# A row softmax over 32,768 columns: half rows moved in one 64 KB transfer per partition instead of two of 32 KB

## The chip, the core and the metric

The kernel runs on one core of one Trainium2 chip. The core has a vector engine (DVE), a scalar engine (ACT) and a sync engine (SP) that are used here, and 16 DMA engines that move data between HBM, where input and output lie, and the core's on-chip memory, which has 128 partitions. TensorE does nothing in this kernel, and GpSimd writes four constants at the start. The metric is device time in microseconds (us) of one execution.

## The reference

```python
def setup_inputs():
    batch, seq, vocab = 16, 256, 32768
    return {"logits": np.random.randn(batch, seq, vocab).astype(np.float32), "temperature": 1.0}

def reference(logits, temperature):
    scaled = logits / temperature
    scaled = scaled - scaled.max(axis=-1, keepdims=True)
    exp_scaled = np.exp(scaled)
    return (exp_scaled / exp_scaled.sum(axis=-1, keepdims=True)).astype(np.float32)
```

There are 16 x 256 = 4,096 rows of 32,768 float32. The input is 536.87 MB and so is the output, and each has to cross between HBM and the core once.

## The kernel before

A row is cut into two halves of 16,384 elements (`_SPLIT = 2`), and each half takes one partition. So 128 partitions hold 64 rows; such a group of 64 rows is called a *tile* below, and there are 64 of them (g = 0 to 63). A half row is 64 KB.

A tile is moved in two *chunks* (`_CW = 8192`, so C = 2): each chunk is 128 partitions x 8,192 elements, 32 KB per partition, 4,096 KB (4 MiB) in all. Each chunk has a buffer of its own, and there are six (`_BUFS = 6`), 6 x 32 = 192 KB of each partition.

For each tile the kernel does three things.

- `exps`: for each *piece* of a chunk (`_PIECE = 8192`, so a piece is a whole chunk), DVE takes the negated maximum of the piece in each partition (L107), then ACT replaces the piece by exp(x - that maximum) in place and adds up the sum in the same pass (L114). Each piece is scaled by its own maximum, so ACT can begin on a piece before the rest of the row is there.
- `factors`: ten or so tiny instructions turn the maxima and sums of the pieces into one factor per piece. The two halves of a row lie in neighbouring partitions, so the partial results are exchanged between partitions (L84, L87). ACT does one tiny exp (L131), and DVE does the rest (L129 to L150).
- `scales`: each piece is multiplied by its factor in place, the first `_DVE_SHARE = 0.5` of it on DVE (L160) and the rest on ACT (L163).

In the last tile the pieces are 4,096 elements in any case. In the first and the last tile the loads go in parts of 16 KB per partition (`_LAST_DMA = 4096`), and in the last tile the stores too.

All transfers are issued by SP, on one queue, in the order that the list `order` at the end of the kernel gives: first as many loads as there are buffers, then a store of chunk 0, and from there store of chunk i, load of chunk i + 5, store of chunk i + 1, and so on (with `_BUFS = n`, load i + n - 1 follows store i). SP works through this list strictly in order. A store (L75) waits until DVE and ACT have scaled the chunk, and a load (L64) waits until the store that last read its buffer has landed. A transfer that waits holds everything behind it on SP. DVE and ACT work through their own lists, tile after tile, in the same manner.

Of the kernel before, what the change touches and what calls it, by code (L numbers as in the profile page):

```python
# [6 lines left out]


_SPLIT = 2
_CW = 8192  # L10
_BUFS = 6
_PIECE = 8192
_LAST_DMA = 4096
_DVE_SHARE = 0.5


@with_exitstack
# [211 lines left out]
```

## Time and profile before

| | |
|---|---|
| time, median of 3 runs | 2494.52 us (2493.96 to 2495.61) |
| the profiled execution's own time | 2495.61 us |
| its span, first to last instruction | 2493.8 us |
| DVE busy | 1487.4 us (60%) |
| ACT busy | 1405.0 us (56%) |
| read from and written to HBM | 536.87 MB each |
| mean rate of the DMA engines | 431 GB/s |
| a 4,096 KB store, issue to landing, median | 38.2 us |
| a 4,096 KB load, issue to landing, median | 29.0 us |

The span is 1.8 us shorter than the time of the same execution; the rest lies before its first and after its last instruction. The profile's page gives each engine's busy time, the busy share of the DMA engines in 40 slices of the span, the chain of work that ended last, followed back from the end, and groups of instructions by line of the kernel with the number of them, the busy time, the mean duration of one, and the idle time before them. The trace behind it also has a record for every packet of the DMA engines (its size, start and duration) and for each of the 16 landings of a transfer, one from each DMA engine.

### The profile page before, as it was taken

The numbers are of one execution on the slowest core, as the hardware profiler recorded it, in microseconds if no ns is written. First come the engines' busy times: TensorE is split into PE (matmuls) and PEld (weight loads), VectorE is DVE, ScalarE is ACT, GpSimd is POOL, SyncE is SP. The second block draws the span as 40 slices with busy tenths as digits, with TensorE's granted clock in tenths as the row PEclk, the third lists the DMA queues.
The fourth block names the chain that finished last, engine by engine and source line by source line (L and its number), as shares of the span: only waits on it lengthen the run. The fifth ranks groups of instructions, "written<-read, shape, count | busy, mean of one in ns | idle before, by whom it ended". The sixth has DMA issues, their size and how long they took to land.

```text
span 2493.8 us, 2234 instructions
## 1 busy us (share of the span) xinstructions
DVE 1487.4 (60%) x964; ACT 1405.0 (56%) x455; POOL 0.2 (0%) x4
## 2 busy tenths in 40 slices
DVE  7655565556655566555665566655666566655663
ACT  5665554655556555565555655555546555465553
POOL 0000000000000000000000000000000000000000
DMA  9999999999999999999999999999999999999998
GB/s 412 433 430 432 429 431 432 433 433 434 433 434 432 435 432 435 432 435 431 436 431 435 432 434 433 434 433 433 433 433 433 433 433 434 434 433 434 432 431 368
DMA packets 37745, 1073.90 MB, mean 431 GB/s; under 512 B 4192, under 2 KB 4192, under 8 KB 4192
## 3 DMA queue, kind: packets, MB, share of 16 engines
q1 hardware_dynamic: 37728, 1073.76, 99.9%
q14 instruction: 17, 0.14, 0.0%
HBM read 536.87 MB, written 536.87 MB: 431 GB/s over the span
## 4 chain that ended last, share of the span: by engine, by line
DMA 96%; SPq 1%; ACT 1%; DVE 1%; issue 1%; ACTq 0%
DMA out_dram<-xs 93%; DMA xs<-in_logits_dram 2%; SPq L64 1%; DVE nm L107 1%; ACT xs L163 1%; ACT xs L114 0%; ACTq L224 0%; SPq L75 0%; DVE f L150 0%; ACT ee L131 0%; DVE rS L149 0%; DVE Sh L87 0%; DVE ttj L138 0%; DVE Sh L84 0%; DVE Sh L138 0%
## 5 line engine op out<-in xcount | busy, mean ns | idle before, releaser
L114 ACT ACTIVATE xs<-xs,nm 128x8192 f32<-128x8192 f32 (+1 forms) x130 | 912.1, 7016 | 972.4 <-DVE nm L107 972.4
L107 DVE TENSOR_REDUCE nm<-xs 128x1 f32<-128x8192 f32 (+1 forms) x130 | 1111.6, 8551 | 527.3 <-DMA xs<-in_logits_dram 527.3
L163 ACT ACTIVATE xs<-xs,f 128x4096 f32<-128x4096 f32 (+1 forms) x130 | 468.1, 3648 | 71.4 <-DVE f L150 71.4
L160 DVE TENSOR_SCALAR xs<-xs,f 128x4096 f32<-128x4096 f32 (+1 forms) x130 | 295.7, 2318 | 3.7 <-DVE f L150 1.8
L138 DVE CUSTOM_DVE_ANT_0 ttj<-ee,ssum 128x2 f32<-128x2 f32 x64 | 10.3, 161 | 423.8 <-ACT ee L131 423.8
L114 ACT ACTIVATION_READ_ACCUMULATOR xs<-xs,nm 128x1 f32 x130 | 24.2, 186 | 0.0
L131 ACT ACTIVATE ee<-nm,nMh 128x2 f32<-128x2 f32 x64 | 17.9, 280 | 0.0
L150 DVE TENSOR_SCALAR f<-ee,rS 128x2 f32<-128x2 f32 x64 | 14.6, 229 | 2.2
L149 DVE RECIPROCAL rS<-Sh 128x1 f32<-128x1 f32 x64 | 10.5, 164 | 2.2
L87 DVE TENSOR_TENSOR nMh<-nMh 128x1 f32<-128x1 f32 x64 | 10.2, 160 | 2.2
L87 DVE TENSOR_TENSOR Sh<-Sh 128x1 f32<-128x1 f32 x64 | 10.2, 160 | 2.2
L129 DVE TENSOR_REDUCE nMh<-nm 128x1 f32<-128x2 f32 x64 | 9.9, 155 | 2.2
L84 DVE STREAM_SHUFFLE nMh<-nMh 128x1 f32<-128x1 f32 x64 | 9.7, 151 | 0.0
L84 DVE STREAM_SHUFFLE Sh<-Sh 128x1 f32<-128x1 f32 x64 | 9.7, 151 | 0.0
L114 ACT ACT_TABLE_LOAD x1 | 1.3, 1283 | 12.9 <-DMA xs<-in_logits_dram 12.9
L138 DVE DVE_READ_ACCUMULATOR2_ANT Sh<- 128x1 f32 x64 | 5.3, 84 | 0.0
L84 DVE LOAD_MASK_SELECT Sh<-Sh x64 | 0.9, 14 | 2.8
L84 DVE LOAD_MASK_SELECT nMh<-nMh x64 | 0.9, 14 | 2.7
L210 POOL MEMSET const-bfloat16-1.0<- 128x1 bf16 x1 | 0.1, 102 | 0.0
L210 POOL MEMSET const-uint8-127<- 128x1 uint8 x1 | 0.1, 102 | 0.0
L210 POOL MEMSET const-float32-0.0<- 128x1 f32 x1 | 0.1, 99 | 0.2 <-issue 0.2
L210 POOL MEMSET const-float32-1.0<- 128x1 f32 x1 | 0.1, 99 | 0.0
## 6 DMA issues: line engine op xcount, KB each, us to landing
out_dram<-xs SPq DMA_DIRECT2D x126, 4096.0 KB, 38.2
xs<-in_logits_dram SPq DMA_DIRECT2D x124, 4096.0 KB, 29.0
xs<-in_logits_dram SPq DMA_DIRECT2D x8, 2048.0 KB, 22.3
out_dram<-xs SPq DMA_DIRECT2D x4, 2048.0 KB, 26.7
```

The costliest lines, as they stand in the source:

```text
L64: nc.sync.dma_start(out=xs[:, s : s + n], in_=x[g * P : (g + 1) * P, c * CW + s : c * CW + s + n],)
L84: nc.vector.stream_shuffle(out=v[:, j + 1 : j + 2], in_=v[:, j : j + 1], mask=mask)
L87: nc.vector.tensor_tensor(out=v[:, j + 1 : j + 2], in0=v[:, j : j + 1], in1=v[:, j + 1 : j + 2], op=op,)
L107: nc.vector.tensor_reduce(out=nm[:, k : k + 1], in_=xs[:, s : s + n], axis=X, op=A.max, negate=True)
L114: nc.scalar.activation(out=xs[:, s : s + n], in_=xs[:, s : s + n], func=Exp, bias=nm[:, k : k + 1], scale=inv_t, accum_out=ssum[:, k : k + 1],
L129: nc.vector.tensor_reduce(out=nMh[:, 0:1], in_=nm, axis=X, op=A.min)
L131: nc.scalar.activation(out=ee, in_=nm, func=Exp, bias=nMh[:, n_rounds : n_rounds + 1], scale=-1.0,)
L138: nc.vector.tensor_tensor_reduce(out=ttj, in0=ee, in1=ssum, scale=1.0, scalar=0.0, op0=A.mult, op1=A.add, accum_out=Sh[:, 0:1],)
L149: nc.vector.reciprocal(out=rS, in_=Sh[:, n_rounds : n_rounds + 1])
L150: nc.vector.tensor_scalar_mul(out=f, in0=ee, scalar1=rS)
L160: nc.vector.tensor_scalar_mul(out=xs[:, s : s + cut], in0=xs[:, s : s + cut], scalar1=f[:, k : k + 1])
L163: nc.scalar.activation(out=xs[:, s + cut : s + n], in_=xs[:, s + cut : s + n], func=Copy, scale=f[:, k : k + 1],)
```

## The change

Four constants change. A chunk becomes a whole half row: 16,384 elements, 64 KB per partition, 8,192 KB per transfer, so a tile is one chunk (C = 1). There are three buffers of 64 KB in place of six of 32 KB, the same 192 KB. A piece becomes 4,096 elements, so a chunk has four pieces, each with its own maximum, sum and factor. DVE scales 0.625 of each piece (2,560 elements) and ACT the other 1,536.

The parts of 16 KB in the first and last tile stay as long as they were, but there are four to the chunk now; and since a piece is also 4,096 elements, the first maximum of the first tile can start once the first part has landed. With three buffers, the load that follows store i in SP's list is that of chunk i + 2.

```diff
-_CW = 8192
-_BUFS = 6
-_PIECE = 8192
+_CW = 16384
+_BUFS = 3
+_PIECE = 4096
 _LAST_DMA = 4096
-_DVE_SHARE = 0.5
+_DVE_SHARE = 0.625
```

## The prediction, made before the changed kernel had run

> **What bounds the kernel now.** I read the busy shares and the slices first, then the chain, then the waits, then the two ends.
>
> ```profile
> DVE 1487.4 (60%) x964; ACT 1405.0 (56%) x455; POOL 0.2 (0%) x4
> ...
> DMA  9999999999999999999999999999999999999998
> GB/s 412 433 430 432 429 431 432 433 433 434 433 434 432 435 432 435 432 435 431 436 431 435 432 434 433 434 433 433 433 433 433 433 433 434 434 433 434 432 431 368
> ...
> q1 hardware_dynamic: 37728, 1073.76, 99.9%
> ...
> DMA 96%; SPq 1%; ACT 1%; DVE 1%; issue 1%; ACTq 0%
> ```
>
> No compute engine is busy for more than 60% of the span, while the one DMA queue keeps its 16 engines busy for 99.9% of it, and the chain that ended last is 96% transfers. The rate is flat at about 433 GB/s, except in the first slice and the last. So only three things can move the time: the cost of a byte on a DMA engine, a hole in its queue, and the two ends.
>
> ```profile
> ACT xs L114 <- DVE nm L107: 972.4, 128, 12.2
> DVE nm L107 <- DMA xs<-in_logits_dram: 527.3, 65, 12.9
> ...
> SPq L64 <- DMA out_dram<-xs: 2246.9, 122, 19.6
> SPq L75 <- DVE xs L160: 73.4, 4, 39.7
> ```
>
> Among the waits, DVE waits for loads, and SP spends 2246.9 us waiting for a store to free a buffer; stores waited for DVE only 4 times. Compute is always early.
>
> ```profile
> 2.00:3.00 1.00, 0.00 (x0) 0.00 (x0) 0.00 (x0) 1.00 0.38 147
> 3.00:4.00 1.00, 0.00 (x0) 0.00 (x0) 0.00 (x0) 1.00 1.01 426
> ...
> 2470.00:2480.00 10.00, 0.00 (x0) 0.00 (x0) 0.00 (x0) 1.00 1.00 429
> 2480.00:2485.00 5.00, 0.00 (x0) 0.00 (x0) 0.00 (x0) 1.00 0.69 295
> 2485.00:2490.00 5.00, 0.00 (x0) 0.00 (x0) 0.00 (x0) 1.00 0.18 79
> 2490.00:2494.00 4.00, 0.00 (x0) 0.00 (x0) 0.00 (x0) 1.00 0.04 16
> ```
>
> Each row here is a stretch of the span; the last two columns are the share of the DMA engines that are busy and the rate. All 16 are busy from 3 us to 2480 us. Then they run out one after another: the landings of the very last store are at 2482.4 to 2482.9 us on eight engines, 2485.5 to 2486.6 on five, then 2488.4, 2489.2 and 2492.9. The slowest engine is 10.5 us behind the fastest, and it alone sets the end.
>
> **What a packet costs.** Each transfer gives each DMA engine 8 rows (128 / 16) as 8 packets, and one 4-byte packet for the semaphore. From start to start on one engine, the packet records give medians of 607 ns for 16 KB and 1209 ns for 32 KB, and means without the stalled ones of 607.07 and 1209.39. So 16 KB more cost 602.32 ns, and a packet costs 607.07 - 602.32 = 4.75 ns whatever its size. The semaphore's packet takes 5.89 ns. Check: an engine has 250 x 8 = 2,000 packets of 32 KB, 12 x 8 = 96 of 16 KB and 262 semaphores, 2418.8 + 58.3 + 1.5 = 2478.6 us; the fastest engines run from 2 to 2482.4 us, and stalls are the rest.
>
> **The change, part by part.**
>
> *Larger rows.* 62 + 63 = 125 transfers of 64 KB rows replace 250, and the 12 of 16 KB rows stay. Each engine has 1,000 packets fewer, if a 64 KB row is one packet: 1,000 x 4.75 = 4.75 us. 125 semaphores fewer: 125 x 5.89 ns = 0.74 us. Sum -5.5 us, on the path, as every DMA engine is saturated. No row shows a 64 KB packet. From below: it is cut into two of 32 KB, and only 0.74 us is saved; from above: the straight line through 16 and 32 KB, 5.5. I take the line, which two sizes support.
>
> The Trainium skill (DMA: Bandwidth & Descriptors, "Anatomy of one DMA") has a fixed 2.0 us for each DMA beside its bytes. By that rule 125 transfers fewer would be worth up to 250 us; the record of 5.89 ns between back-to-back transfers says that the fixed part is latency, hidden while the queue holds work, so I don't take it.
>
> *The lag of the slowest engine*, 10.5 us. Its first 6 us are there by 460 us, from stalls of single packets where the queue passes from a load to a store (769 ns the longest at 60 us, 369 at 129 us, up to 1,225 at 306 us); once the engines are out of step the stalls nearly stop. The remaining 4.5 us come as about 0.35 us on one engine or another every 310 us, which is 256 packets of 32 KB. Changed: half as many switches, but what ends the stalls is being out of step, so I leave the 6. The later part is halved if it goes by packets (-2.2) and stays if it goes by time (0); I take -1.1, the middle. Bounds for the whole lag: it can fall to 5 us (half, by transfers) or grow by 7 (see the rivals).
>
> *Compute between landing and store.* Now the store of a whole tile waits for all of this, after the load has landed: 4 maxima of 4,096 (4 x 4.414 = 17.7 us, from the last tile's rows), the last exp and its sum (3.71 + 0.19 = 3.9), the factors (2452.6 to 2454.0 us in the last tile: 1.4), the scales. DVE's 2,560 elements lie between 1.282 us (2,048) and 2.350 (4,096): 1.55; ACT's 1,536 by the line through 1.990 and 3.701: 1.56; four pieces 6.2. Sum 29.2, and with SP's issue 0.4 and 1.0 from issue to first packet (0.73 to 1.75 us at the start) 30.6 us. The cover: after the load of tile i the queue still holds store i - 1 and load i + 1, 2 x 19.35 = 38.7 us (a 4 MiB chunk takes 9.67). So 8.1 us are spare on the slowest engine, 8.1 less the lag on a faster one. An engine 10 us ahead runs dry for 2 us in a tile, and that only narrows the lead. Cost 0, hidden under 38.7 us of transfers; if this cover fell short, each us would be paid 62 times. The load behind it, i + 2, needs store i - 1, which lands 19.35 us after load i, and store i, issued at 29.6: not late either. Nothing else is on SP, and DVE and ACT take the next tile when it lands, 38.7 us after this one.
>
> The skill (Perfetto Trace Analysis, "Optimization Strategy") warns that gaps repeating on the saturated engine can mean too few buffers or too large tiles. By that, three buffers would bring a gap in each of 62 tiles; the 8.1 us spare say none on the slowest engine.
>
> *More instructions.* 256 maxima x 4.414 = 1130 us and 256 scales x 1.55 = 397 on DVE, about 1,600 with the small ones; ACT 256 x (3.708 + 0.186 + 1.56) + 18 = 1,414. Both under the 2,480 of the DMA engines: 0.
>
> *The ends.* First store: tile 0's fourth part lands at about 22.7 us, then 4.4 + 3.9 + 1.4 + 6.2, so 38.6 us, and the six 4 MiB of loads keep the queue full till 60: 0. The last tile is loaded in four parts, so only the last maximum follows its landing: 4.4 + 3.9 + 1.4 + 1.6 + 1.4 = 12.7 us to the first store's first packet, under store 62 with 19.35: 0.
>
> Sum: 2495.6 (the profiled execution, 1.1 above the median) - 5.5 - 1.1 = 2489.0; against the median, 2487.9.
>
> **The rivals.**
>
> *A, the 64 KB row is cut in two packets.* Nothing in the trace shows either. Saved 0.74, with the lag as it is: 2493.8.
>
> *B, the lag falls with the number of transfers.* For it: the stalls lie at switches between load and store, halved from 127 to 64. Against: they stopped by themselves. Lag 5.2: 2494.5 - 5.5 - 5.3 = 2483.7.
>
> *C, the lag or the stalls grow enough to eat the saving.* Longer packets that collide stall longer. +5 us on the lag: 2494.
>
> *D, slower: the engines stay in step.* The early engines run dry while store i is waited for, start again together, and the stalls at the switch never stop. At 129 us the longest stall was 0.37 us; at 63 switches 23 us, less the 10.5 already paid, less 5.5: +7, so 2501.5. It decides from a stall of (10.5 + 5.5) / 63 = 0.25 us for the slowest engine at each switch. Against: only engines over 8 us ahead run dry, and the slowest never does.
>
> **How the numbers follow.** Under about 0.2% (5.0 us) is what a measurement of this kernel can tell from no change; faster means below 2489.5, slower above 2499.5. Forecast 0.42, with 2484.3 to 2491.5 as its own range: 2494.5 - 5.5 with the two bounds of the late lag (0 and -2.2), and 2.5 us either way for the first 6 us of it, my estimate from single stalls of up to 1.2 us; A 0.12, B 0.23, C 0.12, D 0.11. Faster: 0.7 of the forecast's 0.42, and B, 0.52. Slower: D and a little of C, 0.13. Same: 0.35. The range goes from just below B, 2482, to 2497.5, between C and D.
>
> **What would show it.** Right: packets of 65,536 bytes about 2,414 ns apart, half as many; a DMA share of 9 in every slice; about 434 GB/s in the middle; the store's issue about 29.5 us after the tile's first maximum; SP's time mostly in waits for DVE and ACT before stores. Wrong: packets of 32 KB still (A), a last store that lands within 6 us on all engines (B), windows in mid span whose DMA share is under 0.99 at every tile, with stalled packets to the end (D).

## The result, and the profile after

The changed kernel takes 2504.49 us (median of 4 runs, 2502.32 to 2508.87), beside 2494.24 for the kernel before in the same comparisons. The ratio is 1.0043, with a 95% interval of 1.0026 to 1.0061. It is slower by 0.4%, where the prediction's sum gave 2487.9 us and its range ended at 2497.5. The profiled execution took 2506.49 us, with a span of 2504.7. Among the experiments below, one of the twelve executions of the kernel with more instructions, the profiled one at 2544 us, was in a slower state, and it and its profile are left out.

The page of the changed kernel, with the lines that answer to those shown of before: busy times, the 40 slices, the DMA queue and the instruction queue, the chain.

```profile
DVE 1579.7 (63%) x1216; ACT 1368.7 (55%) x833; POOL 0.2 (0%) x4
...
DMA  9999999999999999999999999999999999999998
GB/s 419 434 426 433 429 436 434 436 434 433 435 434 434 429 428 433 433 434 422 433 422 431 434 423 432 433 422 434 429 425 434 423 433 432 423 433 432 423 422 375
...
q1 hardware_dynamic: 19728, 1073.75, 99.8%
q14 instruction: 20, 0.16, 0.0%
...
DMA 74%; DVE 14%; ACT 10%; SPq 1%; issue 0%; ACTq 0%; another core or an unknown queue 0%
```

The DMA engines are still busy all the time (99.8%), and the number of packets has nearly halved. But the rate is no longer flat. It is 434 to 436 GB/s in half of the first sixteen slices, a little better than before, and from then on every second or third slice falls to 422 or 423. The loss is in the later part of the run, it comes back tile after tile, and it doesn't show as idle time: the packets themselves take longer. The chain has changed too. Before, it was 96% transfers; now a quarter of it is DVE and ACT, because the load of a tile, its compute, its store and the load behind that store now follow each other in a loop.

SP's waits in the changed kernel say the same: it waits for compute before nearly every store (us in total, times, longest us).

```profile
SPq L75 <- DVE xs L160: 2385.2, 67, 38.7
```

The DMA issues by line in the kernel before (number, KB each, median us from issue to landing):

```profile
out_dram<-xs SPq DMA_DIRECT2D x126, 4096.0 KB, 38.2
```

and in the changed kernel, where the page gives no KB for these two:

```profile
out_dram<-xs SPq DMA_DIRECT2D x63, 29.8
xs<-in_logits_dram SPq DMA_DIRECT2D x62, 49.1
```

This is where a reader could have been warned. A store took 38.2 us from its issue to its landing before, of which its own 4 MiB are 9.7, so it was put into the queue some 28.5 us before the DMA engines needed it. Now it takes 29.8 us, of which its own 8 MiB are 19.3, so it is put there only about 10.5 us ahead. I call this the *lead*. It is measured on the slowest DMA engine; an engine that runs ahead has that much less.

The timeline of the changed kernel shows the lead at one tile (start us, us, engine, line, operation):

```profile
1516.43 0.33 SPq L75 DMA_DIRECT2D out_dram<-xs  x1
...
1526.84 17.40 DVE L107 TENSOR_REDUCE nm<-xs 128x1 f32<-128x4096 f32 x4 [10.53 <-DMA xs<-in_logits_dram]
...
1555.41 0.33 SPq L75 DMA_DIRECT2D out_dram<-xs  x1
```

The load has landed on the last engine at 1526.84, when DVE starts; the store is issued at 1555.41, 28.57 us later. Two transfers of a tile take 38.64 us while nothing stalls, so the lead is 38.64 - 28.57 = 10.07 us.

The packet and landing records of the changed kernel show when things turn. A *stall* is the time by which a packet took longer than the usual one of its size, and stalls are summed over the 16 engines; the *lag* is that of the slowest engine behind the fastest.

| | 400 to 900 us | 900 to 1000 us | 1400 to 2400 us |
|---|---|---|---|
| packets' stalls per 100 us, before | 3.8 falling to 0.1 us | 0.0 us | 0.0 to 0.7 us |
| packets' stalls per 100 us, after | 1.6 to 4.0 us | 9.4 us | 12 to 23 us |
| lag, before | 5.8 to 7.2 us | 7.2 us | 8.5 to 10.5 us |
| lag, after | 4.3 to 8.2 us | 8.7 us | 8.5 to 9.5 us, no longer growing |
| a tile, before (fastest engine) | 38.72 us | 38.72 us | 38.73 us |
| a tile, after (fastest engine) | 38.64 us | turning | 39.09 us |

Up to 900 us the changed kernel gains 0.08 us in each tile on its fastest engine, as forecast. Then the lag passes about 8.2 us, with 1.9 us of the lead left for the fastest engine (and 12 to 14 of the 16 engines land within 1 us of the fastest; in the kernel before it is 8 or 9), and from there each tile costs 0.41 to 0.45 us more, on every engine alike: between 1000 and 2400 us each of the 16 engines has some 14 to 18 us of stalls.

### The profile page after: what moved, and what is told of

Its sections match the earlier page's. It is cut to its first block, busy times and chain, and to the rows that moved or that the text cites. A ratio compares the mean times of both kernels' runs of the same rounds, so it can differ in the third digit from the quotient of the medians.

```text
span 2504.7 us, 2498 instructions
## 1 busy us (share of the span) xinstructions
DVE 1579.7 (63%) x1216; ACT 1368.7 (55%) x833; POOL 0.2 (0%) x4
## 3 DMA queue, kind: packets, MB, share of 16 engines
q1 hardware_dynamic: 19728, 1073.75, 99.8%
## 4 chain that ended last, share of the span: by engine, by line
DMA 74%; DVE 14%; ACT 10%; SPq 1%; issue 0%; ACTq 0%; another core or an unknown queue 0%
DMA xs<-in_logits_dram 72%; DVE nm L107 13%; ACT xs L163 7%; ACT xs L114 3%; DMA out_dram<-xs 2%; SPq L75 1%; DVE xs L160 0%; DVE f L150 0%; ACT ee L131 0%; DVE rS L149 0%; DVE Sh L87 0%; DVE Sh L84 0%; DVE ttj L138 0%; ACTq L224 0%
## 5 line engine op out<-in xcount | busy, mean ns | idle before, releaser
L107 DVE TENSOR_REDUCE nm<-xs 128x1 f32<-128x4096 f32 x256 | 1113.7, 4412 | 661.6 <-DMA xs<-in_logits_dram 661.6
L114 ACT ACTIVATE xs<-xs,nm 128x4096 f32<-128x4096 f32 x256 | 949.1, 3708 | 1032.9 <-DVE nm L107 1032.9
L163 ACT ACTIVATE xs<-xs,f 128x1536 f32<-128x1536 f32 x256 | 382.3, 1564 | 73.5 <-DVE f L150 73.5
L160 DVE TENSOR_SCALAR xs<-xs,f 128x2560 f32<-128x2560 f32 x256 | 380.2, 1549 | 2.6 <-DVE f L150 0.4
L138 DVE CUSTOM_DVE_ANT_0 ttj<-ee,ssum 128x4 f32<-128x4 f32 x64 | 10.4, 162 | 222.4 <-ACT ee L131 222.4
L114 ACT ACTIVATION_READ_ACCUMULATOR xs<-xs,nm 128x1 f32 x256 | 47.8, 187 | 0.0
L131 ACT ACTIVATE ee<-nm,nMh 128x4 f32<-128x4 f32 x64 | 18.0, 282 | 0.0
L150 DVE TENSOR_SCALAR f<-ee,rS 128x4 f32<-128x4 f32 x64 | 14.7, 229 | 2.2
L149 DVE RECIPROCAL rS<-Sh 128x1 f32<-128x1 f32 x64 | 10.5, 164 | 2.2
L129 DVE TENSOR_REDUCE nMh<-nm 128x1 f32<-128x4 f32 x64 | 10.1, 157 | 2.2
## 6 DMA issues: line engine op xcount, KB each, us to landing
out_dram<-xs SPq DMA_DIRECT2D x63, 29.8
```

Source lines behind the costliest of these rows:

```text
L107: nc.vector.tensor_reduce(out=nm[:, k : k + 1], in_=xs[:, s : s + n], axis=X, op=A.max, negate=True)
L114: nc.scalar.activation(out=xs[:, s : s + n], in_=xs[:, s : s + n], func=Exp, bias=nm[:, k : k + 1], scale=inv_t, accum_out=ssum[:, k : k + 1],
L129: nc.vector.tensor_reduce(out=nMh[:, 0:1], in_=nm, axis=X, op=A.min)
L131: nc.scalar.activation(out=ee, in_=nm, func=Exp, bias=nMh[:, n_rounds : n_rounds + 1], scale=-1.0,)
L138: nc.vector.tensor_tensor_reduce(out=ttj, in0=ee, in1=ssum, scale=1.0, scalar=0.0, op0=A.mult, op1=A.add, accum_out=Sh[:, 0:1],)
L149: nc.vector.reciprocal(out=rS, in_=Sh[:, n_rounds : n_rounds + 1])
```

## The experiments

Two theories stood after this. The *lead theory*: the stalls come because the store is put into the queue too late for the engines that run ahead. The *packet theory*: 64 KB packets stall by themselves once the engines are some us apart.

**Compute made shorter, nothing else.**

```diff
@@ exps
-                out=nm[:, k : k + 1], in_=xs[:, s : s + n], axis=X, op=A.max, negate=True
+                out=nm[:, k : k + 1], in_=xs[:, s : s + n // 2], axis=X, op=A.max, negate=True
```

> The changed kernel, but each of the four maxima of a tile is taken over the first half of its piece only. This leaves out half of the search for the maximum; the result is still the softmax, because any shift cancels, but it would not be safe for every input. A tile's compute gets about 8.8 us shorter and its store is issued that much earlier, while the transfers, their packets and their order stay as they are. Lead theory (in the changed kernel the store is issued 28.6 us after its load has landed on the slowest DMA engine, 10.1 us less the lag ahead of the fastest engine's need of it; when the lag passes about 8 us the fast engines get the next store too late, and stalled packets come back at every tile): the lead is 18.9 us less the lag, so it never runs out; stalled packets under 1 us per 100 us after 500 us, a tile every 38.64 us to the end, and 2488 us (2485 to 2491). Packet theory (packets of 64 KB stall by themselves once some engines are a few us apart): stalls of 12 to 25 us per 100 us from about 1000 us as in the changed kernel, and 2501 to 2508 us.

Measured: 2493.54 us (ratio 1.000, 0.9991 to 1.001; two of the ten runs took 2497.1 and 2503.0 us). The lasting stalls are gone: 0.0 to 1.6 us per 100 us from 600 to 2000 us, and a tile takes 38.64 us to 2350 us. The busy time by stage (the last two columns are DMA share and GB/s) in the changed kernel:

```profile
500.00:900.00 400.00, 248.13 (x191) 215.07 (x131) 0.00 (x0) 1.00 1.00 433
1000.00:1400.00 400.00, 253.63 (x201) 220.68 (x137) 0.00 (x0) 1.00 1.00 430
1400.00:1800.00 400.00, 246.82 (x190) 213.66 (x130) 0.00 (x0) 1.00 1.00 429
1800.00:2200.00 400.00, 255.30 (x192) 217.47 (x132) 0.00 (x0) 1.00 1.00 430
```

and in this run:

```profile
500.00:900.00 400.00, 161.47 (x190) 210.37 (x130) 0.00 (x0) 1.00 1.00 433
1000.00:1400.00 400.00, 163.82 (x192) 212.82 (x132) 0.00 (x0) 1.00 1.00 434
1400.00:1800.00 400.00, 169.30 (x194) 215.89 (x133) 0.00 (x0) 1.00 1.00 434
1800.00:2200.00 400.00, 164.94 (x203) 220.96 (x138) 0.00 (x0) 1.00 1.00 434
```

Same transfers, same packets, same order; only DVE has less to do, on an engine that is busy 63% of the time, and the rate is 434 GB/s instead of 429 to 430. So the packets of 64 KB don't stall by themselves, and the packet theory falls. Two parts of what I expected were wrong. The store is issued 4.0 us earlier and not 8.8, because ACT's four exps become the longest part, so the lead is 14.1 us; and when the lag passes 12 us near 2130 us, the stalls begin here too (2 to 6 us per 100 us). The landing and the store's issue, 24.53 us apart:

```profile
1520.76 8.86 DVE L107 TENSOR_REDUCE nm<-xs 128x1 f32<-128x2048 f32 x4 [14.22 <-DMA xs<-in_logits_dram]
...
1545.29 0.33 SPq L75 DMA_DIRECT2D out_dram<-xs  x1
```

And the time is 2493.5 and not 2488: the lag of the slowest engine reaches 12.8 us where it was 10.5 in the kernel before. Where that comes from is a question of its own, taken up below.

**Packets of 32 KB with the late store.** Loads and stores of the middle tiles in two transfers, the second half worked on first:

```diff
+    def turned(g: int, ps: list) -> list:
+        return ps[2:] + ps[:2] if 0 < g < G - 1 else ps
@@ load
-        for s, n in spans(CW, _LAST_DMA if g in (0, G - 1) else CW):
+        for s, n in spans(CW, _LAST_DMA if g in (0, G - 1) else CW // 2):
@@ store
-        for s, n in spans(CW, _LAST_DMA if g == G - 1 else CW):
+        for s, n in spans(CW, _LAST_DMA if g == G - 1 else CW // 2):
@@ exps and scales
-        for j, (s, n) in enumerate(ps):
+        for j, (s, n) in turned(g, list(enumerate(ps))):
@@ exps
-            nc.vector.tensor_reduce(
+            tc.keep_in_program_order(
+                nc.vector.tensor_reduce(
...
```

> The changed kernel with all packets of 32 KB: loads and stores of the middle tiles go in two transfers of 32 KB per partition each, and the pieces of the second half are worked on first. So DVE starts only when the whole tile has landed, and no store is issued before the whole tile is scaled: the lead stays that of the changed kernel, 10.1 us less the lag, with the packets of the kernel before. Lead theory: the lasting stalls come back once the lag passes about 8 us, stalls of 10 us and more per 100 us late in the run, and the time is above the kernel before by 8 to 20 us (2502 to 2514). Packet theory: no lasting stalls, 2492 to 2497 us as the kernel before.

Measured: 2506.73 us (ratio 1.0053, 1.0036 to 1.007). The profiled run was the slowest of its four, 2514.74 us; the others took 2505.0 to 2508.2. The store is issued 28.57 us after the landing, as in the changed kernel:

```profile
1531.05 17.40 DVE L111 TENSOR_REDUCE nm<-xs 128x1 f32<-128x4096 f32 x4 [10.78 <-DMA xs<-in_logits_dram]
...
1559.62 0.82 SPq L78 DMA_DIRECT2D out_dram<-xs  x2
```

And the stalls return with the packets of the kernel before: 17 us per 100 us from 900 us on, when the lag has passed 8.8 us, and 11 to 25 us after that. The stages of this run:

```profile
500.00:900.00 400.00, 249.05 (x192) 216.03 (x132) 0.00 (x0) 1.00 1.00 432
1000.00:1400.00 400.00, 250.56 (x200) 219.93 (x135) 0.00 (x0) 1.00 1.00 428
1400.00:1800.00 400.00, 250.00 (x193) 216.96 (x133) 0.00 (x0) 1.00 1.00 428
```

This and the first run together: the size of the packet doesn't bring the stalls, and the lateness of the store does.

**Only the stores, or only the loads, in halves.**

```diff
@@ store
-        for s, n in spans(CW, _LAST_DMA if g == G - 1 else CW):
+        for s, n in spans(CW, _LAST_DMA if g == G - 1 else CW // 2):
```

> The changed kernel, but each tile but the last is stored in two transfers of 32 KB per partition; loads stay at 64 KB. The first store waits for the first two pieces only, so it is issued about 3.0 us earlier. Lead theory: the lead for the first half is 13 us less the lag, which stays under 11: no lasting stalls, 500 packets of 4.75 ns and 63 semaphores more than with 64 KB stores (2.7 us), so 2491 us (2488 to 2494). Packet theory: half of the packets are still of 64 KB, so about half of the loss stays, 2497 to 2503 us.

Measured: 2506.53 us (ratio 1.0045, 1.003 to 1.006): a miss for the lead theory as I had put it. The lag, which I took to stay under 11 us, reached that at about 980 us on several engines, and then stayed near 11.5, with the first half's lead at 13 us. That part fits. But there were 4 to 9 us of stalls per 100 us from 200 us on, long before the lead was used up (6 to 19 after 1000 us), and eight engines fell behind instead of three. Why stores in halves do this is not explained by the lead, and stays open.

```diff
@@ load
-        for s, n in spans(CW, _LAST_DMA if g in (0, G - 1) else CW):
+        for s, n in spans(CW, _LAST_DMA if g in (0, G - 1) else CW // 2):
```

> The changed kernel, but each tile but the first and last is loaded in two transfers of 32 KB per partition; stores stay at 64 KB. Two of the four maxima can then be done before the second half has landed, and the store is issued about 20 us after the landing instead of 28.6. Lead theory: the lead is 18 us less the lag, no lasting stalls, 2.7 us more for packets and semaphores than with 64 KB loads, 2491 us (2488 to 2494). Packet theory: 2497 to 2503 us.

Measured: 2496.29 us (ratio 1.0007, 0.9997 to 1.0016). Store issued 19.9 us after the landing, lead 18.8, stalls of 0.1 to 1.2 us per 100 us after 600 us: the lead theory's side. The run also answers a rival of the first one, that the stalls went away there because DVE read less of the on-chip memory. Here DVE does all its work, as in the changed kernel, and they are gone:

```profile
DVE 1585.3 (64%) x1216; ACT 1368.6 (55%) x833; POOL 0.2 (0%) x4
```

The time is 5 us over what I expected, again by the lag, 12.4 us.

**The lead made smaller, and a little larger.**

```diff
-_DVE_SHARE = 0.625
+_DVE_SHARE = 0.375
```

> The changed kernel with a share of 0.375 in place of 0.625 for DVE in the scales: ACT then scales 2,560 elements of each piece, 2.42 us by the rows instead of 1.56, so a tile's compute is about 3.7 us longer, its store is issued that much later, and the lead is 6.4 us less the lag instead of 10.1. Transfers and packets stay. Lead theory: the lasting stalls begin when the lag passes about 4.5 to 5 us, which is near 500 us and not near 900; the lag then stays under about 6 us instead of 9; some 10 to 12 more tiles pay 0.37 us, so 2508 us (2505 to 2514). Rival (a lag of 8 us is what sets the stalls off, whatever the lead): they begin near 900 us, lag capped near 9, 2502 to 2508 us.

Measured: 2512.40 us (ratio 1.0071, 1.0058 to 1.0084). The store is issued 31.98 us after the landing, so the lead is 6.66 us:

```profile
1530.55 17.40 DVE L107 TENSOR_REDUCE nm<-xs 128x1 f32<-128x4096 f32 x4 [12.52 <-DMA xs<-in_logits_dram]
...
1562.53 0.33 SPq L75 DMA_DIRECT2D out_dram<-xs  x1
```

The stalls begin between 400 and 500 us (9.5 us per 100 us there, 14 to 26 after), with a lag of 4.75 us; the lag then stays between 5 and 6.5 us. Its stores' median from issue to landing is 26.5 us, 7.2 us more than their own 19.3:

```profile
out_dram<-xs SPq DMA_DIRECT2D x63, 26.5
```

```diff
@@ exps
-                out=nm[:, k : k + 1], in_=xs[:, s : s + n], axis=X, op=A.max, negate=True
+                out=nm[:, k : k + 1], in_=xs[:, s : s + n * 13 // 16], axis=X, op=A.max, negate=True
```

> The changed kernel with each maximum taken over 13/16 of its piece; this leaves out 3/16 of the search for the maximum, as before a shift that cancels. Compute is about 3.3 us shorter, so the whole 64 KB store is issued as early as the first half was in the run with stores in halves: lead 13.3 us less the lag. Lead theory: no lasting stalls until the lag passes about 11.5 us, which the run with half the maxima reached at about 2100 us; 2494 to 2497 us, stalls under 2 us per 100 us between 700 and 2000. Rival (13 us of lead are too few, as the store-halves run may be read): stalls of 5 us and more per 100 us all along, 2500 to 2507 us.

Measured: 2504.64 us (ratio 1.0037, 1.0024 to 1.005), a miss in time. Lead 12.7 us (issue 25.94 us after the landing). From 200 to 1200 us the stalls are under 5 us per 100 us, and from 1500 us on 13 to 24. The mechanism was as expected, but the lag got to 10.9 us at 1360 us, where I had counted on 2100, so the loss began earlier. The point from which it costs can now be read from five runs:

| run | lead | lag when the stalls set in | left of the lead |
|---|---|---|---|
| share 0.375 | 6.7 us | 4.75 us (430 us) | 1.9 us |
| changed kernel | 10.1 us | 8.2 us (890 us) | 1.9 us |
| 32 KB, late store | 10.1 us | 8.8 us (870 us) | 1.3 us |
| 13/16 of the maxima | 12.7 us | 10.9 us (1360 us) | 1.8 us |
| half of the maxima | 14.1 us | 12.0 us (2130 us) | 2.1 us |

In these five runs what sets the stalls off is not a lag of a certain size but 1.3 to 2.1 us left of the lead. The run with stores in halves doesn't fit: its stalls were there with much more left. In the kernel before, an issue took about 1.0 us to its first packet at the start of the run, so by this estimate the point is where the fastest engine gets its next transfer only just before it is through with the last.

How many engines move together is not the condition. In the changed kernel 13 or 14 of the 16 land within 1 us of the first from 300 to 900 us already, with stalls of only 1.6 to 4.0 us per 100 us.

**Where the lag comes from.** In the runs without lasting stalls the slowest engine falls back in steps, every 310 us in the kernel before and every 233 or 272 us in the run with loads in halves. Beside each step the trace has a packet of 8 KB on the instruction queue. 310 us are 8 tiles, and DVE runs 16 instructions per tile, so one such packet goes with 128 instructions (233 and 272 us are 6 and 7 tiles of 20). DVE's program has 1,037 instructions before and 1,287 in the changed kernel (four maxima and four scales per tile instead of two and two), which makes 8 and 10 fetches. I tested this from both sides.

```diff
+    pad = spool.tile([P, 16], fp32, tag="pad", name="pad")
...
@@ factors
+        for j in range(16):
+            tc.keep_in_program_order(nc.vector.memset(pad[:, j : j + 1], 0.0))
```

> The kernel before with 16 one-column memsets more on DVE per tile, so that DVE's program has 2,061 instructions instead of 1,037; they write a scratch tile that nothing reads, and take about 1 us of DVE's idle time per tile. Fetch theory (the slowest DMA engine falls behind because it also carries DVE's instructions, one packet of 8 KB for each 128 of them, and each such packet costs it about 0.65 us): 16 fetches instead of 8, one every 155 us, the last store's lag grows from 10.5 to about 15.5 us, and the time by 5 us, to 2499.5 us (2498 to 2501.5). Rival (the lag grows with time or with bytes): 2494.4 us, within 1.5.

Measured: 2499.81 us, the median of eleven runs, beside 2494.91 for the kernel before: 4.9 us more by the medians, as expected. Nine of the eleven lie between 2499.1 and 2502.2; the other two took 2511.0 and 2518.1, which nothing here explains, and raise the ratio, which goes by the means, to 1.0031 (1.0018 to 1.0045), 7.7 us. The steps themselves are not shown for this run.

```diff
-_PIECE = 4096
+_PIECE = 8192
@@ load
-        for s, n in spans(CW, _LAST_DMA if g in (0, G - 1) else CW):
+        for s, n in spans(CW, _LAST_DMA if g in (0, G - 1) else CW // 2):
```

> The run with loads in halves, but with pieces of 8,192 elements, so that DVE has 16 instructions per tile as the kernel before and not 20 (1,037 in all, not 1,287). Lead about 15 us less the lag, so no lasting stalls. Fetch theory: 8 fetches of DVE's instructions instead of 10, at about 0.9 us each: 1.8 us less than that run's 2496.3, so 2494.5 us (2492.5 to 2496), and the slowest engine falls back about every 310 us, not every 250. Rival (the lag goes by time): 2496.3 us.

Measured: 2494.64 us (ratio 0.9999, 0.999 to 1.0008). Each against the runs of the kernel before in its own comparison, this is 0.3 us faster and the run with 20 instructions per tile 1.9 us slower, so 2.2 us apart where 1.8 were expected. The steps come at 1076.9, 1387.4, 1698.0, 2008.5 and 2319.1 us, 310 us apart, each a packet 0.64 to 0.65 us too long and some 0.3 us for the fetch itself.

In every run looked at, the fetch takes 0.30 us in which its engine moves no data, but the packet behind it is too long by different amounts: 0.36 us in the kernel before, 0.55 in the run with 32 KB packets and the late store, 0.61 to 0.64 with half of the maxima, 0.64 to 0.65 here. The size of the packets doesn't decide this, since those of 32 KB behind the fetches are both the least (before) and the most delayed (here). In the kernel before the packet belongs to a store, in the other three to a load; no run tests whether that is the reason. The instruction queue's packets and bytes, in the run with loads in halves:

```profile
q14 instruction: 21, 0.17, 0.0%
```

and here:

```profile
q14 instruction: 16, 0.13, 0.0%
```

So the steps of the lag come by the number of instructions that are fetched, and not by time. This run has no lasting stalls, and is as fast as the kernel before, no faster.

## Why the prediction was wrong, step by step

- *Larger rows, -5.5 us.* Right. A 64 KB row is one packet (16,000 of 65,536 bytes in the trace), 2,414 ns apart. A tile takes 38.64 us instead of 38.72 while nothing stalls, 0.083 us x 62 = 5.2 us. Rival A, with two packets, did not occur. Leaving out the cited 2.0 us for each transfer was right too, since two transfers fewer per tile gained 0.08 us. (The section cited for it is on transfers that GpSimd issues; here SP issues them.)
- *The lag of the slowest engine, -1.1 us.* Wrong in sign. I had taken the steps every 310 us, "which is 256 packets of 32 KB", for something that goes by packets or by time. They are fetches of DVE's program, and the change made that longer; each also cost more, about 0.9 us where it was 0.66. The prediction's "about 0.35 us on one engine or another" missed the 0.30 us of the fetch itself, and the steps that make the lag fall on one engine, the slowest. In the run with half the maxima, where this shows with few stalls, the lag is 12.8 us instead of 10.5: +2.3. In the changed kernel itself it stayed at 8.5 to 9.5 us, as the fast engines were held back too.
- *Compute between landing and store, cost 0.* This is the step that failed. Its sizes were good: 29.2 us to the end of the scales, measured 28.57 to the store's issue. Its conclusion was not: "An engine 10 us ahead runs dry for 2 us in a tile, and that only narrows the lead." The runs show something else. From 1000 to 2400 us the engines hardly run dry (some 11 us of gaps over all 16), but their packets stall by 244 us around the changes between loads and stores, on the slowest engine as on the others, and every tile pays. From about 950 us to the end, 38 tiles at 39.07 instead of 38.64 us are 16.3 us.
- *More instructions, 0.* Their busy time was hidden, as said (DVE 1579.7 us for about 1,600, ACT 1368.7 for 1,414). Their fetching was not in my sum at all.
- *The ends, 0.* No loss on the slowest engine. The fast engines waited for the last tile's stores, so the very last store landed within 4.3 us on all engines. The prediction had given that as the sign of rival B, and here it came without B's gain.

Together: -5.2 + 16.3 = +11.1 us, beside 10.9 between the two profiled executions (2506.49 and 2495.61). The rest, more stalls early on against a lag that stays under 10 us, is within 2 us of nothing.

Rival D, "the engines stay in step", named the place and nearly the price: it was to decide from 0.25 us per switch, and gave 2501.5. It measured 0.43 us in each tile from 950 us on. I gave it 0.11, on the argument that "the slowest never does" run dry. That is true and beside the point. What also differs: 13 or 14 of the 16 engines were in step from early on, without the loss, and it began only when the lag had used up the lead. Of the signs given for D, stalled packets to the end came, and a DMA share under 0.99 did not: it stayed at 0.99 to 1.00.

What is not settled is why a packet stalls then. In the changed kernel 198 of the 244 us of stalls between 1000 and 2400 us lie on the last packet of a transfer, and engines with 10 us of work in their queues have them too. Three quarters of those near a change lie where a store gives way to the next load (about 164 us), which had been in the queue for some 20 us, and only about 54 us where the load gives way to the late store. So the stalls are mostly not a wait for that store. That its lateness sets them off is shown by the runs, with the run with stores in halves as the exception; what happens inside the DMA engines is not.

## What to carry to other kernels

When a kernel is bound by transfers, look for how long before its need a transfer is issued: the median time from issue to landing, less the transfer's own duration, in the list of DMA issues. Here larger transfers in fewer buffers bought almost nothing per byte (0.2%) and ate that lead; in five of the six runs with such stalls, the lead had to exceed the lag between the fastest and the slowest DMA engine by some 2 us, and at the end of the run, not at its beginning. What held the lead was to split the loads and let compute start on the first part, or to shorten the compute, even on an engine that is idle a third of the time. That only won back the loss: no run was clearly faster than the kernel before.

## What the runs showed of the hardware that was not expected

- A packet on a DMA engine costs about 4.75 ns whatever its size, and 602 ns for each 16 KB: 607, 1,209 and 2,414 ns from start to start for 16, 32 and 64 KB.
- The instruction stream of an engine is fetched in packets of 8 KB by DMA engines that also carry data. Each fetch of DVE's program, one for 128 instructions, cost its DMA engine 0.66 us in the kernel before and 0.85 to 0.95 us in the other runs looked at, with packets of 32 KB as with those of 64 KB. The end of the kernel waits for the slowest DMA engine, and 16 idle instructions more per tile cost 4.9 us of 2,495 without using any engine's time that mattered.
- A DMA share of 0.99 or 1.00 in every stretch says that packets are on the engines, not that they move at full speed: the changed kernel had 1.00 at 429 GB/s and at 434.
